# A sorted gather-transform-scatter on one core: 16-bit bank offsets for TensorE's registers, output matmuls four columns later, and no copy behind the sort

## The chip, the cores and the metric

The kernel runs on one core of one Trainium2 chip. The metric is the device time in microseconds (us) of one execution; before the change its median over three runs is 989.48 us, with 987.77 us the lowest and 990.58 us the highest.

A core has a matrix engine (TensorE, "PE" in the profile; its weight loads are listed apart as "PEld"), a vector engine (VectorE, "DVE"), a scalar engine (ScalarE, "ACT"), GpSimd ("POOL") and SyncE ("SP", used here to issue DMAs). Each engine takes its instructions in order from a queue of its own; a small processor in front of each engine, its sequencer, reads that queue and itself executes the instructions that work on registers. Engines wait for one another through semaphores. PSUM is the memory that TensorE writes into, SBUF the memory that all engines read and write.

## What is computed

There are 4096 nodes with 256 features each and 262,144 edges. Each edge adds the transformed features of its source node to its destination node; each node also gets its own transform.

```python
def reference(nodes, edges_src, edges_dst, w_msg, w_self):
    N, D = nodes.shape
    self_out = nodes @ w_self
    src_feat = nodes[edges_src]
    msg = src_feat @ w_msg
    agg = np.zeros((N, D), dtype=np.float32)
    np.add.at(agg, edges_dst, msg)
    return (self_out + agg).astype(np.float32)
```

## The kernel before

The kernel turns the scatter into dense matrix products. It has three stages.

**Transform.** `Y = nodes @ w_msg` is computed once per block of 128 nodes (line 182) and kept in SBUF in bfloat16 as 32 blocks of 128 rows. The transposed nodes stay in SBUF as `XT`.

**Sort.** The 262,144 edges are packed as one number each: the group of 512 destination nodes (a "segment", 8 of them), then the block of 128 source nodes (32 of them), then the destination within the segment and the source within the block. A bitonic network sorts these keys in `_run_sort`. Two layouts are used, "A" (tiles `XA`) and "B" (tiles `XB`), each with two buffers; every pass reads one buffer and writes the other, so that an index `cur` tells which of the two holds the live data. A pass is two VectorE instructions, a minimum (line 574) and a maximum (line 575). Changing the layout goes through TensorE transposes and PSUM (`switch_A_to_B`, `switch_B_to_A`). After the last pass the function makes sure that the result lies in buffer 0 of each layout (lines 598 to 604), because the code behind it names `XA[0]` and `XB[0]`. Layout A has 111 passes, an odd number, so that its live buffer is the second one and the copy on line 599 runs; layout B has 60, so that its own copy never appears in the program. The last `switch_A_to_B` stands between the two.

**Count and apply.** The sorted edges form 2048 columns of 128. For each column, VectorE has built two one-hot matrices (function `onehots`, line 307, 16 columns at a time): one for the source within its block (`e_oh`, 128 wide) and one for the destination within a window of 96 nodes (`d_oh`). Their product on TensorE (`count_mm`, line 323) counts edges between each source and destination, and adds into PSUM. A (segment, block) pair is called a run; there are 256 runs, 8 columns each on average, and six of them share PSUM at a time as a ring of six banks of 512 columns (`ring`). Where in the ring a column's 96-wide window lies is known only after the sort: it is the column's "offset". The offsets are computed on VectorE as `poff` (line 238), go to DRAM (`pd`, line 239) and come back as one row of 2048 numbers on one partition (`poffs`, line 240). TensorE's sequencer loads eight of them into registers with one instruction (line 396, `TENSOR_LOAD` in the profile), and every count matmul has an instruction of its own that turns its register into a PSUM address (`FUSED_REGOPS` in the profile, also put down to line 323).

The order of TensorE's queue in this stage is written out by hand under `tc.manual_schedule()`. For column `c`: at `c % 16 == 0` the one-hots are requested; a run's first columns may need an additional count matmul (`head_mm`, one for each run); at `c % 8 == 0` the eight offsets are loaded; then comes the count matmul. When all columns that can belong to run `r` are past (`8*r + 7 + MARG <= c`, with `MARG` 10), ScalarE copies the run's bank to SBUF as bfloat16 (`evac`, line 339), and `LAG` columns later the four output matmuls of the run follow (`apply_run`, line 365), which multiply the counts by the block of `Y` and add into `out_ps`. The first run of a segment has eight more matmuls for the node's own transform (line 360), and the last one copies `out_ps` to `o_sb` on ScalarE (line 372) and sends it to DRAM from SyncE's queue.

```python
            if c % 8 == 0:
                regs = [nc.tensor.alloc_register(f"po{c}_{i}") for i in range(8)]
                nc.tensor.load(regs, poffs[0:1, c:c + 8])
            off = nc.tensor.snap(
                regs[c % 8], donate=True, min_val=0, max_val=RING * SEGW - W
            )
            count_mm(ring[:, bass.ds(off, W)], e, d, ci, False)
            while nev < NRUN and (8 * nev + 7 + MARG <= c or c == NCOL - 1):
                evac(nev)
                todo.append((c + LAG, nev))
                nev += 1
            while todo and (todo[0][0] <= c or c == NCOL - 1):
                apply_run(todo.pop(0)[1])
```

Everywhere else a scheduler puts VectorE's, ScalarE's and the DMA instructions in order. Around the end of the sort VectorE's queue also holds a check that the sorted data fits the fixed windows (lines 416 to 446: `bad`, `bcol`, `bsum`, `flag`), and the index `cidx` (line 264) with which GpSimd fetches the columns for the head matmuls (line 273).

Of the kernel before, what the change touches and what calls it, by code (L numbers as in the profile page):

```python
# [9 lines left out]
P = 128  # L10
FP32 = mybir.dt.float32
BF16 = mybir.dt.bfloat16
I32 = mybir.dt.int32
I64 = mybir.dt.int64

ALU = mybir.AluOpType
AX = mybir.AxisListType
# [4 lines left out]
SL = 16  # L22
RING = 6
MARG = 10
LAG = 10
NRUN = 256
SENT = float((1 << 24) - 1)

# [7 lines left out]
def _view3(ap: bass.AP, inner: int):  # L36
    return ap.rearrange("p (a b) -> p a b", b=inner)
# [3 lines left out]
def kernel(  # L41
# [9 lines left out]
    nc = tc.nc  # L51
# [4 lines left out]
    NCOL = E // P  # L56
# [3 lines left out]
    NSTAGE = 18  # L60
    JBITS = 11
    G16 = NCOL // P
# [3 lines left out]
    meta = ctx.enter_context(tc.tile_pool(name="meta", bufs=1))  # L66
    dram = ctx.enter_context(tc.tile_pool(name="dram", bufs=1, space=bass.MemoryType.DRAM))
# [2 lines left out]
    xs_dram = dram.tile([NCOL, P], FP32, name="xs_dram")  # L70
    kd = dram.tile([1, NCOL + 1], FP32, name="kd")
    gd = dram.tile([1, NCOL], FP32, name="gd")
    pd = dram.tile([1, NCOL], I32, name="pd")
    fd = dram.tile([1, P], FP32, name="fd")
    rd = dram.tile([1, NCOL + 64], I32, name="rd")

    ident = const.tile([P, P], FP32, name="ident")
# [8 lines left out]
    XA = [sortp.tile([P, NCOL], FP32, name=f"XA{i}") for i in range(2)]  # L86
    XB = [sortp.tile([P, NCOL], FP32, name=f"XB{i}") for i in range(2)]

    HC = NCOL // 2
    for h in range(2):  # L90
        d64 = XB[0][:].bitcast(I64)
        s64 = XB[1][:].bitcast(I64)
        nc.sync.dma_start(
# [14 lines left out]
            out=key, in0=dlo, scalar=128.0, in1=slo, op0=ALU.mult, op1=ALU.add  # L108
        )
        nc.vector.scalar_tensor_tensor(  # L110
            out=key, in0=dhi, scalar=float((1 << 21) - (1 << 16)), in1=key,
# [3 lines left out]
            out=key, in0=shi, scalar=float((1 << 16) - P), in1=key,  # L115
# [24 lines left out]
        out=hbase[:], in0=hbase[:], scalar1=float(SEGW), scalar2=None, op0=ALU.mult  # L140
# [6 lines left out]
        out=thr[:], in0=thr[:], scalar1=float(SEGW), scalar2=-0.5, op0=ALU.mult, op1=ALU.add  # L147
# [31 lines left out]
    for t in range(T):  # L179
        y_ps = psum_y.tile([P, D], FP32, name="y_ps", tag="y_ps", bufs=2)  # L180
        for k in range(2):
            nc.tensor.matmul(  # L182
                out=y_ps[:], lhsT=XT[:, k, t * P:(t + 1) * P], rhs=wcat[:, 2 + k, :],
# [2 lines left out]
        nc.scalar.copy(out=Y[:, t, :], in_=y_ps[:])  # L186

    psum_sort = tc.alloc_tile_pool(name="psum_sort", bufs=1, space=bass.MemoryType.PSUM)
    _run_sort(nc, psum_sort, XA, XB, ident, NCOL, NSTAGE, JBITS, G16)
    srt = XA[0]  # L190
    lane = XB[0]


    k16 = meta.tile([P, G16], FP32, name="k16")
# [9 lines left out]
    gb = meta.tile([P, G16], FP32, name="gb")  # L204
    sl = meta.tile([P, G16], I32, name="sl")
    wr = meta.tile([P, G16], I32, name="wr")
    poff = meta.tile([P, G16], I32, name="poff")
    gball = meta.tile([P, NCOL], FP32, name="gball")
    poffs = meta.tile([1, NCOL], I32, name="poffs")
    junk = meta.tile([P, NCOL], BF16, name="junk")  # L210
    cnt = meta.tile([P, 2], FP32, name="cnt")
    cidx = meta.tile([P, 2], I32, name="cidx")
# [8 lines left out]
        out=ex[:], in0=dl[:], scalar1=float(W - SEGW), scalar2=0.0, op0=ALU.add, op1=ALU.max  # L221
# [9 lines left out]
        out=wr[:], in0=sl[:], scalar1=float(RING), scalar2=float(-RING * SEGW),  # L231
# [3 lines left out]
        out=wr[:], in0=sl[:], scalar=float(SEGW), in1=wr[:], op0=ALU.mult, op1=ALU.add  # L235
# [20 lines left out]
    for h in range(2):  # L256
        nc.scalar.activation(
            out=junk[:], in_=gball[:], func=ACTF.Sign, bias=thr[:, h:h + 1], scale=-1.0,
# [3 lines left out]
        out=cnt[:], in0=cnt[:], scalar1=0.5, scalar2=float(NCOL // 2 - 1), op0=ALU.mult, op1=ALU.add  # L262
    )
    nc.vector.tensor_scalar(
        out=cidx[:], in0=cnt[:], scalar1=0.0, scalar2=None, op0=ALU.max
# [5 lines left out]
    for h in range(2):  # L271
        xh = meta.tile([P, P], FP32, name=f"xh{h}")
        nc.gpsimd.indirect_dma_start(
            out=xh[:], out_offset=None, in_=xs_dram[:, :],
# [61 lines left out]
    def evac(r):  # L336
        at = ohp.tile([P, SEGW], BF16, name="at", tag="at", bufs=4)
        b = (r % RING) * SEGW
        ins = nc.scalar.copy(out=at[:], in_=ring[:, b:b + SEGW]).ins  # L339
        tc.declare_no_dep(  # L340
            ins, group="count", keep=[last_mm[0]], reason="disjoint banks by static schedule"
        )
        tc.add_manual_dep(ins, last_mm[0].name, DEP, reason="run complete")
        tc.add_to_no_dep_group("evac", ins)
        evac_of[r] = ins
        at_of[r] = at
# [28 lines left out]
    with tc.manual_schedule():  # L375
# [5 lines left out]
        for c in range(NCOL):  # L381
# [19 lines left out]
# [4 lines that stand above are left out]
# [18 lines left out]
        out=hh[:], in0=rho[:], scalar1=float(SEGW), scalar2=float(SEGW), op0=ALU.mult, op1=ALU.add  # L423
    )
    nc.vector.scalar_tensor_tensor(
        out=v[:], in0=gn[:], scalar=1.0, in1=hh[:], op0=ALU.add, op1=ALU.min
# [3 lines left out]
        out=bad[:], in0=v[:], scalar=float(W), in1=bad[:], op0=ALU.is_gt, op1=ALU.add  # L430
# [3 lines left out]
        out=bad[:], in0=v[:], scalar=float(W - 1), in1=bad[:], op0=ALU.is_gt, op1=ALU.add  # L434
# [4 lines left out]
        out=bad[0:1, 0:1], in0=gi[0:1, 0:1], scalar=float(W - 1), in1=bad[0:1, 0:1],  # L439
# [16 lines left out]
def _any_edges(tc, edges_src, edges_dst, out, XT, Y, wcat, ident, N, D, E, T):  # L456
    nc = tc.nc
    with tc.tile_pool(name="g_sb", bufs=1) as sb, tc.tile_pool(
# [14 lines left out]
        with tc.For_i(0, E, P) as i:  # L473
            s64 = sb.tile([P, 1], I64, name="g_s64")
            d64 = sb.tile([P, 1], I64, name="g_d64")
            nc.sync.dma_start(s64[:], edges_src[bass.ds(i, P)].unsqueeze(1))
# [34 lines left out]
def _run_sort(nc, psum, XA, XB, ident, NCOL, NSTAGE, JBITS, G16):  # L511

    cur = {"A": 0, "B": 0}

    def buf(lay):
        return XA[cur[lay]][:, 0:NCOL] if lay == "A" else XB[cur[lay]][:, 0:NCOL]

    def other(lay):
        return XA[1 - cur[lay]][:, 0:NCOL] if lay == "A" else XB[1 - cur[lay]][:, 0:NCOL]

    def flip_live(lay):
        cur[lay] = 1 - cur[lay]

    def evac(out_ap, in_ap, g):
        if g % 2 == 0:
            nc.scalar.copy(out=out_ap, in_=in_ap)  # L526
        else:
            nc.vector.tensor_copy(out=out_ap, in_=in_ap)

    def switch_A_to_B():  # L530
        src = buf("A")
        dst3 = buf("B").rearrange("q (p g) -> q p g", g=G16)
        for g in range(G16):
            tp = psum.tile([P, P], FP32, name="tp_sw", tag="tp", bufs=4)
            nc.tensor.transpose(tp[:], src[:, g * P:(g + 1) * P], ident[:])  # L535
            evac(dst3[:, :, g], tp[:], g)

    def switch_B_to_A():
        src3 = buf("B").rearrange("q (p g) -> q p g", g=G16)
        dst = buf("A")  # L540
        for g in range(G16):
            tp = psum.tile([P, P], FP32, name="tp_sw2", tag="tp", bufs=4)
            nc.tensor.transpose(tp[:], src3[:, :, g], ident[:])
            evac(dst[:, g * P:(g + 1) * P], tp[:], g)

    def flip(lay, blo, bhi):
        x = buf(lay)
        if lay == "A":
            assert blo <= JBITS - 1 and (bhi is None or bhi <= JBITS - 1)
            base_lo = blo  # L550
        else:
            assert blo >= 7
            base_lo = blo - 7
            if bhi is not None:
                assert bhi == blo + 1
        if bhi is None:
            per = 1 << (base_lo + 1)
            reg = _view3(x, per)[:, :, (1 << base_lo):per]
        else:
            per = 1 << (base_lo + 2)  # L560
            reg = _view3(x, per)[:, :, (1 << base_lo):(3 << base_lo)]
        nc.vector.tensor_scalar(out=reg, in0=reg, scalar1=-1.0, scalar2=None, op0=ALU.mult)

    def cpass(lay, fb):
        src = buf(lay)
        dst = other(lay)
        per = 1 << (fb + 1)
        s3 = _view3(src, per)
        d3 = _view3(dst, per)
        lo_s = s3[:, :, 0:(1 << fb)]  # L570
        hi_s = s3[:, :, (1 << fb):per]
        lo_d = d3[:, :, 0:(1 << fb)]
        hi_d = d3[:, :, (1 << fb):per]
        nc.vector.tensor_tensor(out=lo_d, in0=lo_s, in1=hi_s, op=ALU.min)  # L574
        nc.vector.tensor_tensor(out=hi_d, in0=lo_s, in1=hi_s, op=ALU.max)  # L575
        flip_live(lay)

    for s in range(1, NSTAGE + 1):
        if s <= JBITS - 1:
            if s == 1:  # L580
                flip("A", 1, None)
            else:
                flip("A", s - 1, s)
            for b in range(s - 1, -1, -1):
                cpass("A", b)
        else:
            switch_A_to_B()
            if s == NSTAGE:
                flip("B", NSTAGE - 1, None)
            else:  # L590
                flip("B", s - 1, s)
            for b in range(s - 1, 6, -1):
                cpass("B", b - 7)
            switch_B_to_A()
            for b in range(6, -1, -1):
                cpass("A", b)

    if cur["A"] != 0:
        nc.vector.tensor_copy(out=XA[0][:, 0:NCOL], in_=XA[cur["A"]][:, 0:NCOL])
        cur["A"] = 0  # L600
    switch_A_to_B()
    if cur["B"] != 0:
        nc.vector.tensor_copy(out=XB[0][:, 0:NCOL], in_=XB[cur["B"]][:, 0:NCOL])
        cur["B"] = 0


# [28 lines left out]
```

## Time and profile before

| | |
|---|---|
| median of three runs | 989.48 us |
| the profiled execution, its own time | 990.0 us |
| its span, first to last instruction | 988.2 us |
| mean granted TensorE clock | 0.846 of full speed |
| PE busy | 417.9 us (42%), 3730 matmuls |
| DVE busy | 782.6 us (79%) |
| ACT busy | 222.0 us (22%) |
| DMA | 18.03 MB, mean 18 GB/s |

The page has six parts: busy time per engine, the span in 40 slices, the DMA queues, the chain of work that ended last, the costliest groups of instructions, and the DMA issues. The sort fills the span up to about 518 us, with VectorE busy nearly all the time. The count stage runs from about 548 us to the end. In a group's row stand line, engine, operation, destination and sources, then count, busy time and mean duration of one in nanoseconds, and last the idle time of the engine just before these instructions and what ended it; "issue" is idle time that ended without any wait that the profile shows.

### The profile page before, as it was taken

Reading aid. Unit: us, or ns where it says so; the run is one execution under the profiler, and the core shown is the slowest. Engines: PE = TensorE matmul, PEld = TensorE weight load, DVE = VectorE, ACT = ScalarE, POOL = GpSimd, SP = SyncE. Lnnn points to the kernel's source line nnn. Section 1 sums busy time; section 2 is a strip of 40 time slices with the busy share of each in tenths; the row PEclk is TensorE's granted clock in tenths of the full one; section 3 lists DMA queues with packets and bytes.
Section 4 is the critical chain, followed back from the end, with each engine's and each line's share of the span. In section 5 each row is a group of like instructions: output and inputs, shape, how many; then the busy total and the mean of one; then the engine's idle time right before and its main releaser. Section 6 shows DMA issues by size and latency. Waiting matters only on the chain.

```text
span 988.2 us, 11711 instructions
## 1 busy us (share of the span) xinstructions
PE 417.9 (42%) x3730; PEld 317.9 (32%) x3730; DVE 782.6 (79%) x851; ACT 222.0 (22%) x449; POOL 14.3 (1%) x24
## 2 busy tenths in 40 slices
PE   0033301131111120202012677777777777777775
PEld 0000001121111120101011566565565656566654
DVE  3999999989999989898995986767766666767640
ACT  0011101021010110101003233333333333333333
POOL 4000000000000000000000000000000000000000
PEclk9999999999555555555555699999999999999999
DMA  8611100000000000000003000000000000000000
GB/s 228 132 26 26 24 0 0 1 1 0 0 0 0 0 1 0 0 0 0 0 0 93 1 2 23 1 23 1 1 23 2 23 1 23 2 23 1 23 2 24
DMA packets 25217, 18.03 MB, mean 18 GB/s; under 512 B 11557, under 2 KB 24358, under 8 KB 24390
## 3 DMA queue, kind: packets, MB, share of 16 engines
q1 hardware_dynamic: 19862, 11.59, 3.9%
q0 software_dynamic: 4720, 2.49, 1.9%
q10 hardware_dynamic: 578, 3.16, 0.8%
q8 instruction: 39, 0.64, 0.3%
q14 instruction: 18, 0.15, 0.0%
HBM read 10.12 MB, written 7.37 MB: 18 GB/s over the span
## 4 chain that ended last, share of the span: by engine, by line
DVE 49%; PE 35%; issue 12%; DMA 3%; ACT 0%; DVEq 0%; ACTq 0%; SPq 0%
PE ring L323 18%; PE out_ps L365 10%; DVE XA_85 L574 7%; DVE XA_84 L574 7%; DVE XA_85 L575 7%; DVE XA_84 L575 6%; DVE XB_86 L574 4%; DVE XB_87 L574 4%; DVE XB_87 L575 3%; DVE XB_86 L575 3%; PE tp_sw L535 3%; DVE e_oh L307 2%; DVE d_oh L307 2%; DMA XB_86<-in_edges_dst_dram 2%; DMA fd<-bcol 1%
## 5 line engine op out<-in xcount | busy, mean ns | idle before, releaser
L323 PE MATMUL ring<-d_oh,e_oh 128*128 128x96 bf16 x2304 | 242.3, 206 | 114.9 <-issue 105.0
L307 DVE TENSOR_TENSOR e_oh<-slo_b,jrow 128x2048 bf16<-128x2048 bf16 x128 | 156.5, 1222 | 114.1 <-PE ring L323 114.1
L323 PEld LDWEIGHTS <-e_oh 128*128 128x128 bf16 x2304 | 170.2, 98 | 158.9 <-issue 143.5
L339 ACT CAST at<-ring 128x512 bf16<-128x512 f32 x256 | 150.0, 586 | 289.9 <-PE ring L323 289.9
L365 PE MATMUL out_ps<-Y,at 128*128 128x256 bf16 x1024 | 154.3, 273 | 0.2 <-ACT at L339 0.2
L307 DVE TENSOR_TENSOR d_oh<-rel_b,jrow 128x1536 bf16<-128x1536 bf16 x128 | 121.7, 951 | 0.0
L365 PEld LDWEIGHTS <-at 128*128 128x128 bf16 x1024 | 85.0, 97 | 15.9 <-issue 1.8
L574 DVE TENSOR_TENSOR XA_85<-XA_84 128x1024 f32<-128x1024 f32 x56 | 68.6, 1225 | 2.2
L574 DVE TENSOR_TENSOR XA_84<-XA_85 128x1024 f32<-128x1024 f32 x55 | 67.4, 1225 | 2.2
L575 DVE TENSOR_TENSOR XA_85<-XA_84 128x1024 f32<-128x1024 f32 x56 | 68.3, 1219 | 0.0
L575 DVE TENSOR_TENSOR XA_84<-XA_85 128x1024 f32<-128x1024 f32 x55 | 67.1, 1219 | 0.0
L182 PE MATMUL y_ps<-wcat,XT 128*128 128x256 bf16 x64 | 25.2, 395 | 97.5 <-DMA XT<-nodes_bf_dram 97.5
L535 PE MATMUL tp_sw<-ident,XA_84 128*128 128x128 f32 x80 | 20.6, 432 | 88.1 <-DVE XA_84 L575 68.9
L535 PE MATMUL tp_sw<-ident,XA_85 128*128 128x128 f32 x64 | 15.8, 436 | 93.7 <-DVE XA_85 L575 93.7
L535 PEld LDWEIGHTS tp_sw<-ident,XA_84 128*128 128x128 f32 x80 | 14.1, 192 | 94.5 <-DVE XA_84 L575 70.0
L182 PEld LDWEIGHTS <-XT 128*128 128x128 bf16 x64 | 6.7, 104 | 115.7 <-DMA XT<-nodes_bf_dram 115.7
L535 PEld LDWEIGHTS tp_sw<-ident,XA_85 128*128 128x128 f32 x64 | 11.6, 190 | 97.8 <-DVE XA_85 L575 52.4
L526 ACT COPY XB_86<-tp_sw 128x128 f32<-128x128 f32 x40 | 15.1, 377 | 119.4 <-PE tp_sw L535 116.9
L574 DVE TENSOR_TENSOR XB_87<-XB_86 128x1024 f32<-128x1024 f32 x30 | 36.8, 1225 | 1.0
L574 DVE TENSOR_TENSOR XB_86<-XB_87 128x1024 f32<-128x1024 f32 x30 | 36.8, 1225 | 1.0
L575 DVE TENSOR_TENSOR XB_87<-XB_86 128x1024 f32<-128x1024 f32 x30 | 36.6, 1219 | 0.0
L575 DVE TENSOR_TENSOR XB_86<-XB_87 128x1024 f32<-128x1024 f32 x30 | 36.6, 1219 | 0.0
(478 smaller groups left out, 288.3 us busy)
## 6 DMA issues: line engine op xcount, KB each, us to landing
out_dram<-o_sb SPq DMA_DIRECT2D x16, 256.0 KB, 2.5
XB_87<-in_edges_src_dram ACTq DMA_DIRECT2D x2, 1024.0 KB, 8.7
XB_86<-in_edges_dst_dram SPq DMA_DIRECT2D x2, 1024.0 KB, 8.5
nodes_bf<-in_nodes_dram POOLq DMA_DIRECT2D x1, 2048.0 KB, 20.1
nodes_bf_dram<-nodes_bf SPq DMA_DIRECT2D x1, 2048.0 KB, 8.7
XT<-nodes_bf_dram SPq DMA_TRANSPOSE x64, 2.4
xs_dram<-XA_84 ACTq DMA_DIRECT2D x1, 1024.0 KB
gball<-gd SPq DMA_DIRECT2D x1, 1024.0 KB, 4.7
```

The source lines that it names most:

```text
L182: nc.tensor.matmul(out=y_ps[:], lhsT=XT[:, k, t * P:(t + 1) * P], rhs=wcat[:, 2 + k, :], start=(k == 0), stop=(k == 1),)
L307: tt(out=o[:], in0=val.rearrange("p (g i) -> p g i", i=2).unsqueeze(2).to_broadcast(shp), in1=jrow[:, 0:wid, :].unsqueeze(1).to_broadcast( ...
L323: mm = nc.tensor.matmul(out=ap, lhsT=e[:, ci // 2, :, ci % 2], rhs=d[:, ci // 2, :, ci % 2], start=start, stop=True, skip_group_check=True ...
L339: ins = nc.scalar.copy(out=at[:], in_=ring[:, b:b + SEGW]).ins
L365: nc.tensor.matmul(out=out_ps[:, t, :], lhsT=at[:, t * P:(t + 1) * P], rhs=Y[:, b, :], start=False, stop=(b == T - 1), skip_group_check=True,)
L526: nc.scalar.copy(out=out_ap, in_=in_ap)
L535: nc.tensor.transpose(tp[:], src[:, g * P:(g + 1) * P], ident[:])
L574: nc.vector.tensor_tensor(out=lo_d, in0=lo_s, in1=hi_s, op=ALU.min)
L575: nc.vector.tensor_tensor(out=hi_d, in0=lo_s, in1=hi_s, op=ALU.max)
```

## The change

Three edits are made together. The offsets are kept as 16-bit integers (`poff`, `pd`, `poffs`), so that a load of eight registers reads 16 bytes instead of 32. `LAG` goes from 10 to 14: a run becomes ready for its output matmuls at columns with `c % 8 == 1`, so with 10 they stood behind the count of a column with `c % 8 == 3`, and with 14 they stand behind one with `c % 8 == 7`, directly ahead of the next register load. And `_run_sort` returns the live buffers instead of copying layout A's into buffer 0.

```diff
@@ -12,6 +12,7 @@
 I64 = mybir.dt.int64
+I16 = mybir.dt.int16
@@ -22,7 +23,7 @@
 MARG = 10
-LAG = 10
+LAG = 14
@@ -70,7 +71,7 @@
-    pd = dram.tile([1, NCOL], I32, name="pd")
+    pd = dram.tile([1, NCOL], I16, name="pd")
@@ -186,9 +187,7 @@
-    _run_sort(nc, psum_sort, XA, XB, ident, NCOL, NSTAGE, JBITS, G16)
-    srt = XA[0]
-    lane = XB[0]
+    srt, lane = _run_sort(nc, psum_sort, XA, XB, ident, NCOL, NSTAGE, JBITS, G16)
@@ -204,9 +203,9 @@
-    poff = meta.tile([P, G16], I32, name="poff")
+    poff = meta.tile([P, G16], I16, name="poff")
     gball = meta.tile([P, NCOL], FP32, name="gball")
-    poffs = meta.tile([1, NCOL], I32, name="poffs")
+    poffs = meta.tile([1, NCOL], I16, name="poffs")
@@ -595,13 +594,8 @@
-    if cur["A"] != 0:
-        nc.vector.tensor_copy(out=XA[0][:, 0:NCOL], in_=XA[cur["A"]][:, 0:NCOL])
-        cur["A"] = 0
     switch_A_to_B()
-    if cur["B"] != 0:
-        nc.vector.tensor_copy(out=XB[0][:, 0:NCOL], in_=XB[cur["B"]][:, 0:NCOL])
-        cur["B"] = 0
+    return XA[cur["A"]], XB[cur["B"]]
```

In the changed program TensorE's queue holds the same instructions as before, in the new order. VectorE's queue has one instruction less (the copy); the addition that makes `poff` becomes a plain 16-element one; and the scheduler puts a few small instructions elsewhere: `cidx` goes ahead of seven of the small instructions of the check instead of behind them, and `bsum` goes behind the first dozen one-hot pairs instead of ahead of the first head one-hot. The queues of SyncE, ScalarE and GpSimd keep their order.

## The prediction

> **What bounds the kernel now.** I read the page's busy rows and its chain of waits first, then the rows of groups, then the chain and the timeline of a few microseconds, and last the single lines.
>
> ```profile
> DVE 49%; PE 35%; issue 12%; DMA 3%; ACT 0%; DVEq 0%; ACTq 0%; SPq 0%
> ```
> ```profile
> L323 PE MATMUL ring<-d_oh,e_oh 128*128 128x96 bf16 x2304 | 242.3, 206 | 114.9 <-issue 105.0
> L307 DVE TENSOR_TENSOR e_oh<-slo_b,jrow 128x2048 bf16<-128x2048 bf16 x128 | 156.5, 1222 | 114.1 <-PE ring L323 114.1
> ```
>
> The chain has two halves: VectorE (the sort) and TensorE (the count stage) with 12% of "issue". The count matmuls stand idle 105 us for "issue", that is, for no other engine, while VectorE waits 114 us for them: in the count stage VectorE is not the bound. The chain in the middle of the stage shows the rhythm (start, length, what):
>
> ```profile
> 701.60 0.44 PE out_ps L365 x4
> 702.03 0.22 PE ring L323 x5
> 702.25 0.41 issue
> 702.66 0.57 PE ring L323 x4
> 703.23 0.44 PE out_ps L365 x4
> ```
>
> One run takes 1.63 us: 0.44 for four output matmuls, 0.22 for five counts, a hole of 0.41, 0.57 for four counts. The array needs only 0.44 for the outputs and 9 x 0.044 = 0.40 for the counts (five in 0.22 when they stand ready), 0.84 in all. What fills the rest is in the lines of the sequencer's own instructions (minimum/median/maximum in ns, then first and last start in us; the windows are 700 to 712 us for the second row, one run from 714.1 us for the third):
>
> ```profile
> L396 PEldq TENSOR_LOAD <-poffs x256: 587/591/1332, 548.2 to 977.7; - x128
> ...
> L396 PEldq TENSOR_LOAD <-poffs x8: 587/590/593, 700.2 to 711.8; - x8
> ...
> L323 PEldq FUSED_REGOPS  x8: 37/37/37, 714.2 to 715.0; - x8
> ...
> L451 PEldq TENSOR_LOAD <-flag x1: 307/307/307, 980.9 to 980.9; - x1
> ```
>
> Loads follow each other every (711.8-700.2)/7 = 1.66 us and last 0.59. The eight address instructions behind each start 0.11 to 0.12 apart ((715.0-714.2)/7) although each lasts 0.037, and do so across the four output matmuls as well: output matmuls cost the sequencer nothing that shows. So the sequencer alone has 0.59 + about 0.10 to the first address instruction + 8 x 0.115 + a few hundredths = 1.63, the whole period. The timeline confirms it twice:
>
> ```profile
> 550.90 1.09 PE L323 MATMUL ring<-d_oh,e_oh 128*128 128x96 bf16 x9 [0.58 <-issue]
> 552.56 1.10 PE L323 MATMUL ring<-d_oh,e_oh 128*128 128x96 bf16 x9 [0.57 <-issue]
> ...
> 558.75 0.93 PE L323 MATMUL ring<-d_oh,e_oh 128*128 128x96 bf16 x9
> 559.48 0.88 PE L365 MATMUL out_ps<-Y,at 128*128 128x256 bf16 x4
> 560.20 0.56 PE L323 MATMUL ring<-d_oh,e_oh 128*128 128x96 bf16 x9
> ```
>
> At 551 us there are no output matmuls yet, and the period is 1.66 all the same. At 557 to 561 us the array runs at half clock and is behind; then the hole is gone, but the three loads begun there last 587 to 593 ns: a load neither waits for matmuls that are outstanding nor gets shorter beside them.
>
> **What the Trainium skill says.** "Advanced Engine Details and Errata", Sequencer Loop: engine instructions are pushed into a queue, control instructions run on the sequencer itself; that is what the rows above show. Its Engine Queue Depths gives TensorE 64; the 13 matmuls outstanding at 559.1 us did not fill it. "DMA: Bandwidth & Descriptors", Latency and other measured facts, puts a floor of about 600 ns under a register load; the trace has 590 for eight registers, but 307 for one, so it is no floor. "Runtime: NRT & Kernel Launch", Instruction fetch mechanics, prices a register load from HBM at about 200 ns per register even in bulk; from SBUF the trace has 590/8 = 74. No page says what the element's width does.
>
> **The change part by part.**
>
> *Output matmuls directly ahead of the load.* The same instructions, in the order: nine counts, four outputs, load. The array can do the outputs during the load, but the sequencer must still do its load and its eight address instructions one after the other, and every count waits for its own. The counts that used to pile up behind the outputs and run during the load now come 0.115 apart. The period stays the sum above: I cost the move at 0. A run's copy on ScalarE gets four columns more before its output needs it; it does not wait for that now. The array's 0.84 us fit into any period down to that.
>
> *16-bit loads.* A load then reads 16 bytes instead of 32. The trace does not show such a load. Lower end: the one-register load, 307 ns. Upper end of a harmless outcome: 590. Two readings of 307 and 590: each further register costs (590-307)/7 = 40 ns, and width is nothing; or the load reads memory in blocks, one block for the single register and two for 32 bytes, as 590 is close to twice 307. If the fixed part of a load is between 37 ns (an address instruction) and 100 ns (what passes behind a load), the second block is worth 207 to 270 and each register 2 to 11, and eight registers in one block take 307 + 7 x (2 to 11) = 321 to 384. I take this reading, since 40 ns for each register is a lot for a processor that does a whole address instruction in 37, and the value 370, nearer its careful end: 0.22 us less. All 256 loads are on the path: 256 x 0.22 = 56.3 us. Given back: at half clock (548 to 561 us, clock 0.54) the array needs 1.58 us a run, more than the new 1.41; some five runs at 0.17, 0.8 us.
>
> What is late next? At 1.41 a run VectorE has 2.83 us for 16 columns; its pair takes 2.17 (1.222 + 0.951), 2.0 when pairs overlap (545.79 to 547.79 in the chain), with the heads' share a quarter more: 2.25. ScalarE has 0.59 a run. The array has 0.84. None is the bound.
>
> *The copy at the end of the sort,* and what the scheduler moves with it:
>
> ```profile
> 517.23 1.23 DVE L599 COPY XA_84<-XA_85 128x2048 f32<-128x2048 f32 x1
> ...
> 535.65 0.17 DVE L264 TENSOR_SCALAR cidx<-cnt 128x2 int32<-128x2 f32 x1
> 536.10 1.09 POOL L273 DMA_INDIRECT xh_1583<-xs_dram,cidx  x1 [522.91 <-DVE cidx L264]
> ...
> 545.52 0.27 DVE L445 TENSOR_REDUCE bsum<-brow 1x1 f32<-1x128 f32 x1 [0.36 <-DMA brow<-fd]
> 545.72 1.20 DVE L307 TENSOR_TENSOR e_oh<-hsl,jrow 128x2048 bf16<-128x2048 bf16 x1
> ```
>
> Everything behind the copy waits for it: with its gap 1.26 us (517.23 to 518.49). `cidx`, from which the fetch of the head columns starts, goes ahead of seven small instructions 0.21 apart: 1.4 us earlier, and the chain cidx, fetch, transpose, head one-hots sets when TensorE starts counting. `bsum`, for which VectorE waited 0.36 and which stood ahead of the first head one-hot, goes behind: 0.57 us (545.15 to 545.72). Sum 3.2 us, at least the 1.26. The halved offset transfers (issued at 521.8 and 523.9 us) are wanted at 548.2 and stay hidden. At the end of the run one more output group falls into the last column, where the array waits for ScalarE anyway: 0.
>
> **Sum.** 990.0 (the profiled execution, 1.8 around its span) - 56.3 + 0.8 - 3.2 = 931.3; the median of the runs shown is 0.5 below that execution, so I forecast 931.
>
> **The rivals.**
>
> *Width is nothing* (10%): the load stays at 590. Then only the 3.2 us come: 986. For it: a load that works register by register would scale with their number, and 40 ns is possible. This lies at the limit of 0.3% (3 us, about what a measurement here can tell), so half of it counts as no change.
>
> *The move hides the load* (3%): the hole of 0.41 goes altogether, 256 x 0.41 + 3.2 = 108 us, 882. Against it: the sequencer is in order, and the 551 us rows keep 1.66 without any output matmul.
>
> *16-bit values are not read in blocks* (17%): a load of narrow elements, which must be widened to a register, could go element by element. Place: TensorE's sequencer, line 396. Price: seven further accesses of 200 ns (the runtime page's, and the 207 to 270 above), 307 + 1400 = 1.7 us a load, 1.1 more than now, 256 x 1.1 = 286, to 1273; with 307 for each register it is 2.46 us and 1465. It decides as soon as a load takes more than 590 + 6200/256 = 614 ns. For it speaks that nothing here shows a 16-bit load; against it that 74 ns per register shows that this load does read more than one register at a time.
>
> **How the numbers follow.** The main case has 70%. Its own range: a load of 321 ns gives 918, one of 450 (a widening cost of 10 ns for each register on top) gives 951. The range must leave out no more than 20%: the third rival (17%) and the second (3%) stay out, the first is taken in, and a little is added below: 912 to 990. Faster by over 0.3%: 70 + 3 + 5 = 78%; within 0.3%: 5%; slower: 17%.
>
> **What would show it.** The load's row is the test: about 370 ns right, 590 or more wrong. Loads should follow each other every 1.41 to 1.44 us, the hole before the first count of a run should still stand, now behind the outputs, and the address instructions should still be 0.115 apart. If the period falls below the sum of load and address instructions, I am wrong about the sequencer; if it stays above it, something else (VectorE's one-hots first) has become late. Line 599 should be gone and the first load should begin near 545 us.

## The result, and the profile after

The changed kernel takes 1324.85 us (median of four runs, 1323.69 to 1325.13) against 988.99 us for the kernel before in the same comparison: a ratio of 1.339, with a 95% interval of 1.337 to 1.342. It is slower by 336 us. The profiled execution took 1325.13 us, its span is 1323.4 us.

The rows of groups of the changed kernel, to be held against those of before:

```profile
L306 DVE TENSOR_TENSOR e_oh<-slo_b,jrow 128x2048 bf16<-128x2048 bf16 x128 | 156.7, 1224 | 426.8 <-PE ring L322 426.8
L322 PE MATMUL ring<-d_oh,e_oh 128*128 128x96 bf16 x2304 | 278.2, 247 | 269.3 <-issue 145.8
```

VectorE does the same work as before (156.7 us in this row) but now waits 427 us for TensorE instead of 114. TensorE waits for "issue" in 146 of its 269 us. Most of the rest (116) is put down to `e_oh`, but that is not what it waited for: at 902.16 us, for one, the hole is again 1.03 us, and the one-hot instruction named had ended at 901.55. The sequencer's own lines say what the wait is for. They are the register loads of the whole program, the eight address instructions of one run, and the single-register load of `flag`, each with minimum/median/maximum in ns and then first and last start in us:

```profile
L395 PEldq TENSOR_LOAD <-poffs x256: 1916/1919/2555, 546.3 to 1310.7; - x128
...
L322 PEldq FUSED_REGOPS  x8: 37/37/37, 913.9 to 914.8; - x8
...
L450 PEldq TENSOR_LOAD <-flag x1: 320/320/320, 1315.1 to 1315.1; - x1
```

A 16-bit load of eight registers takes 1919 ns where the 32-bit load took 591. The address instructions are untouched (37 ns, 0.9/7 = 0.13 us apart at this rounding), and a load of one 32-bit register still takes about 0.3 us. The chain of waits in the middle of the stage shows what is left of the rhythm (start, length, what):

```profile
908.13 1.07 PE ring L322 x9
909.20 0.85 PE out_ps L364 x4
910.05 1.03 issue
911.09 0.98 PE ring L322 x8
```

One run takes 911.09 - 908.13 = 2.96 us. The output matmuls do stand ahead of the load, as the change wants, and a part of the load does pass beside them; what sticks out behind them is 1.03 us in which the array has nothing to do. The stage runs at half the array's clock (0.52 between 600 and 1200 us), and that does not set the time: even so the array has run out of work 1.03 us before the next address is ready. The arithmetic closes: 256 loads x (1.919 - 0.591) = 340 us, against 336 measured.

### The profile page after: what moved, and what is told of

Read it like the earlier page. It is cut to its first block, busy times and chain, and to the rows that moved or that the text cites. A ratio compares the mean times of both kernels' runs of the same rounds, so it can differ in the third digit from the quotient of the medians.

```text
span 1323.4 us, 11701 instructions
## 1 busy us (share of the span) xinstructions
PE 600.9 (45%) x3730; PEld 420.8 (32%) x3730; DVE 782.3 (59%) x850; ACT 222.2 (17%) x449; POOL 14.4 (1%) x24
## 4 chain that ended last, share of the span: by engine, by line
DVE 45%; PE 35%; issue 17%; DMA 2%; ACT 0%; POOL 0%; DVEq 0%
PE ring L322 21%; DVE e_oh L306 11%; PE out_ps L364 9%; DVE XA_85 L573 5%; DVE XA_84 L573 5%; DVE XA_85 L574 5%; DVE XA_84 L574 5%; DVE XB_87 L573 3%; DVE XB_86 L573 3%; DVE XB_86 L574 3%; DVE XB_87 L574 3%; PE tp_sw L534 2%; DMA XB_86<-in_edges_dst_dram 1%; PE out_ps L359 1%; DVE d_oh L306 1%
## 5 line engine op out<-in xcount | busy, mean ns | idle before, releaser
L306 DVE TENSOR_TENSOR e_oh<-slo_b,jrow 128x2048 bf16<-128x2048 bf16 x128 | 156.7, 1224 | 426.8 <-PE ring L322 426.8
L322 PE MATMUL ring<-d_oh,e_oh 128*128 128x96 bf16 x2304 | 278.2, 247 | 269.3 <-issue 145.8
L322 PEld LDWEIGHTS <-e_oh 128*128 128x128 bf16 x2304 | 236.9, 117 | 373.4 <-issue 337.5
L364 PE MATMUL out_ps<-Y,at 128*128 128x256 bf16 x1024 | 264.1, 412 | 0.0
L364 PEld LDWEIGHTS <-at 128*128 128x128 bf16 x1024 | 124.5, 137 | 33.7
```

The lines of the kernel that those rows point to most:

```text
L306: tt(out=o[:], in0=val.rearrange("p (g i) -> p g i", i=2).unsqueeze(2).to_broadcast(shp), in1=jrow[:, 0:wid, :].unsqueeze(1).to_broadcast( ...
L322: mm = nc.tensor.matmul(out=ap, lhsT=e[:, ci // 2, :, ci % 2], rhs=d[:, ci // 2, :, ci % 2], start=start, stop=True, skip_group_check=True ...
L364: nc.tensor.matmul(out=out_ps[:, t, :], lhsT=at[:, t * P:(t + 1) * P], rhs=Y[:, b, :], start=False, stop=(b == T - 1), skip_group_check=True,)
```

## The experiments

The expectations name a theory A and its rivals. At first A says only that narrow elements are fetched register by register; ahead of the runs with a spread and a shifted row it is widened: only a contiguous, aligned row of full-width elements is fetched several registers at a time, and anything else goes register by register. The sequencer's sum (load + 0.1 us + eight address instructions) then gives the time.

**One part alone: 16-bit offsets.**

```diff
-    pd = dram.tile([1, NCOL], I32, name="pd")
+    pd = dram.tile([1, NCOL], I16, name="pd")
...
-    poff = meta.tile([P, G16], I32, name="poff")
+    poff = meta.tile([P, G16], I16, name="poff")
...
-    poffs = meta.tile([1, NCOL], I32, name="poffs")
+    poffs = meta.tile([1, NCOL], I16, name="poffs")
```

> The kernel before with the 16-bit offsets alone (poff, pd and poffs as 16-bit integers; LAG stays 10, the copy stays). Theory A (a load of narrow elements fetches each register by an access of its own, 307 + 7 x 230 = 1917 ns, and TensorE's sequencer is the bound): loads of 1917 to 1922 ns, one load every 2.95 us, 1325 to 1330 us in all. Rival B (the narrow load is slow only because the output matmuls now stand directly ahead of it): loads near 590 or below, 930 to 990 us.

It took 1325.75 us against 990.25 for the kernel before, ratio 1.339 (1.337 to 1.341), the ratio of the whole change. Its load line:

```profile
L397 PEldq TENSOR_LOAD <-poffs x256: 1916/1919/2227, 546.6 to 1310.1; - x128
```

The output matmuls stand at their old place here, and the load is just as long. The 16-bit edit is the whole loss; rival B falls.

**The rest of the change without it.** The changed kernel with the three tiles back at 32 bits (LAG 14, no copy):

```diff
-    pd = dram.tile([1, NCOL], I16, name="pd")
+    pd = dram.tile([1, NCOL], I32, name="pd")
...
-    poffs = meta.tile([1, NCOL], I16, name="poffs")
+    poffs = meta.tile([1, NCOL], I32, name="poffs")
```

> The changed kernel with the offsets back at 32 bits: LAG 14 and no copy. Theory A: loads at 590 ns, 1.63 us a run, and only the earlier start of the count stage is left, 2 to 3 us: 985 to 987. Rival C (the move by four columns costs something of its own in the count stage): above 990. Rival D (the move hides the load behind the output matmuls): 880 to 950.

986.27 us against 990.25: ratio 0.9958 (0.9944 to 0.9972), with loads of 590 ns. The size is what theory A expected, but not the place: the first load begins at 548.1 us, where it began before (548.2), and the next two runs divide the gain differently.

**The move alone.**

```diff
-LAG = 10
+LAG = 14
```

> The kernel before with LAG 14 alone. Theory A: no change, 988 to 990, one load every 1.63 to 1.64 us with the hole now behind the output matmuls instead of behind five counts. Rival C: above 992. Rival D: 880 to 950.

986.89 us, ratio 0.9964 (0.9951 to 0.9978): 3.4 us faster, where theory A had nothing. The main point of A holds; the chain of waits of this run:

```profile
702.02 0.44 PE out_ps L365 x4
702.46 0.18 issue
702.64 1.01 PE ring L323 x9
703.65 0.44 PE out_ps L365 x4
```

The hole has shrunk from 0.41 to 0.18 us, as one would hope when work is put beside a load, and the run still takes 703.65 - 702.02 = 1.63 us. What the hole lost came back in the counts: nine now take 1.01, where five that had piled up and four at the sequencer's pace took 0.22 + 0.57 = 0.79. Idle time of the array moved; the sum on the sequencer did not. The 3.4 us come from elsewhere. The load line names a place:

```profile
L396 PEldq TENSOR_LOAD <-poffs x256: 587/590/932, 549.6 to 975.6; - x128
```

The longest load is 932 ns; before it was 1332. Before, seven loads, one at each change of segment, took about 1.2 us, while the output of the last segment leaves (`out_dram<-o_sb`). From the first to the last load 426.0 us pass instead of 429.5; about 2.2 of these 3.5 us lie in the two intervals between loads at each change, the rest is spread over the others. That the loads now meet less of the output transfer fits, but no run separates the transfer from the other work of a change of segment, so this stays an inference. Nor does the move always help there: with 16-bit loads, usually 1.92 us, those at the changes last 2.36 to 2.56 us with `LAG` 14 and 2.20 to 2.23 with `LAG` 10.

**The copy alone.** The kernel before, with `_run_sort` returning the live buffers and nothing else.

```diff
-    if cur["A"] != 0:
-        nc.vector.tensor_copy(out=XA[0][:, 0:NCOL], in_=XA[cur["A"]][:, 0:NCOL])
-        cur["A"] = 0
     switch_A_to_B()
...
+    return XA[cur["A"]], XB[cur["B"]]
```

> The kernel before without the copy at the end of the sort, nothing else; VectorE's queue keeps bsum ahead of the first head one-hot. If the copy stands on the path to the end (prediction): 1.2 us less than before, or more. If the fetches through DRAM behind it set the start of the count stage instead: 0 to 0.7 us less.

989.12 us, ratio 0.9998 (0.9988 to 1.0009): nothing that can be measured. The timeline of this run between the sort and the counts (start, length, engine, line, operation, idle time before):

```profile
517.12 0.17 DVE L216 CAST k16i<-XA 128x16 int32<-128x16 f32 x1
...
534.70 0.32 SPq L442 DMA_DIRECT2D fd<-bcol  x1
...
542.31 0.24 SPq L443 DMA_DIRECT2D brow<-fd  x1
...
545.57 0.27 DVE L444 TENSOR_REDUCE bsum<-brow 1x1 f32<-1x128 f32 x1 [0.82 <-DMA brow<-fd]
545.77 1.20 DVE L306 TENSOR_TENSOR e_oh<-hsl,jrow 128x2048 bf16<-128x2048 bf16 x1
```

The first instruction behind the sort starts 1.37 us earlier (518.49 before), and the transfer of `bcol` is issued 0.87 earlier (535.57 before), but the first head one-hot starts at 545.77 against 545.72. In front of it stands `bsum`, which waits for a round trip through DRAM (`fd`, `brow`): 10.9 us from issue to `bsum` here, 9.95 before. Why the round trip took longer in this execution is open; one trace of each kernel cannot tell. In the changed kernel, and in the run with 16-bit offsets alone, the scheduler puts `bsum` further back (568.1 and 568.2 us); there the first load begins at 546.3 and 546.6 instead of 548.2, without the copy and with it.

**Is it the width of the element or the length of the row?** Loads of four 32-bit registers, 16 bytes like the changed kernel's.

```diff
-            if c % 8 == 0:
-                regs = [nc.tensor.alloc_register(f"po{c}_{i}") for i in range(8)]
-                nc.tensor.load(regs, poffs[0:1, c:c + 8])
+            if c % 4 == 0:
+                regs = [nc.tensor.alloc_register(f"po{c}_{i}") for i in range(4)]
+                nc.tensor.load(regs, poffs[0:1, c:c + 4])
...
-                regs[c % 8], donate=True, min_val=0, max_val=RING * SEGW - W
+                regs[c % 4], donate=True, min_val=0, max_val=RING * SEGW - W
```

> The kernel before with 32-bit loads of four registers each, twice as many loads: 16 bytes a load, as many as the changed kernel reads. Theory A with blocks of 16 bytes (a contiguous 32-bit row is fetched block by block): a load of 310 to 350 ns, two of them and two gaps of 0.1 in place of one, 0.1 to 0.2 us more a run, 1015 to 1040 us. Rival E (width of the row, not of the element, makes a 16-byte load slow): a load of 900 ns or more, over 1200 us. Rival F (each register 40 ns, no blocks): a load of 427 ns, 0.36 us more a run, about 1083 us.

```profile
L396 PEldq TENSOR_LOAD <-poffs x512: 326/328/772, 548.6 to 1023.2; - x171
```

328 ns for four registers, 21 more than for one (7 each), and 262 less than for eight. So three more registers cost 21 ns and the next four 262. That fits blocks of four registers, 16 bytes; no run loads five or six, so the step itself is not seen. A short row is not slow: rivals E and F fall. The time, 1033.97 us (ratio 1.044, 1.043 to 1.046), follows from twice as many loads.

**Is it narrowness, or anything that is not a plain row?** First the same 32-bit values spread out, one every 8 bytes:

```diff
-    poffs = meta.tile([1, NCOL], I32, name="poffs")
+    poffs = meta.tile([1, NCOL, 2], I32, name="poffs")
...
-    nc.scalar.dma_start(poffs[:], pd[0:1, :])
+    nc.scalar.dma_start(poffs[:, :, 0], pd[0:1, :])
...
-                nc.tensor.load(regs, poffs[0:1, c:c + 8])
+                nc.tensor.load(regs, poffs[0:1, c:c + 8, 0])
```

> The kernel before with the 32-bit offsets spread out in SBUF, one every 8 bytes, so that a load's eight values are full width but not contiguous; values and order as before. Theory A in its wide form (block fetches only for a contiguous row of 32-bit elements; anything else goes register by register): loads of 1915 to 1925 ns, about 1325 us. Rival G (only narrow elements go one by one; a strided row is still fetched in 16-byte blocks, four of them): 307 + 3 x 234 + 7 x 7 = 1058 ns, about 1110 us. Rival H (each needed block of 16 bytes costs nothing more, the load stays at 590): 990 us.

Then the plain row, shifted by one element:

```diff
-    poffs = meta.tile([1, NCOL], I32, name="poffs")
+    poffs = meta.tile([1, NCOL + 1], I32, name="poffs")
...
-    nc.scalar.dma_start(poffs[:], pd[0:1, :])
+    nc.scalar.dma_start(poffs[:, 1:NCOL + 1], pd[0:1, :])
...
-                nc.tensor.load(regs, poffs[0:1, c:c + 8])
+                nc.tensor.load(regs, poffs[0:1, c + 1:c + 9])
```

> The kernel before with the row of 32-bit offsets shifted by one element, so that every load starts 4 bytes behind a multiple of 16. Theory A in its wide form with alignment as a condition: 1915 to 1925 ns, about 1325 us. Rival I (unaligned rows are read in three blocks): 307 + 2 x 234 + 7 x 7 = 824 ns, about 1050 us. Rival H: 590 ns, 990 us.

Their load lines, the spread row first:

```profile
L396 PEldq TENSOR_LOAD <-poffs x256: 1920/1926/2217, 554.5 to 1319.3; - x128
```
```profile
L396 PEldq TENSOR_LOAD <-poffs x256: 1929/1933/2228, 548.8 to 1315.8; - x128
```

1926 and 1933 ns, 1333.64 and 1330.17 us (one execution each; the spread row's first load begins 7.9 us later than that of the run with 16-bit offsets alone, and the same 7.9 us lie between their times). Narrow, spread or shifted, a load of eight costs the same, to within 1%. That speaks for one common slow path: 16-bit elements do not have a slow way of their own, they lose the fast one. Rivals G, H and I fall. If each register is fetched on its own there, a further register costs (1919 - 307)/7 = 230 ns; that it is so is argued and not shown, since every slow load here has eight registers.

**Fewer, longer loads.** The second run's kernel with 32 registers per load, and with 16; each 8 in these lines becomes 32 or 16. The edit for 16:

```diff
-            if c % 8 == 0:
-                regs = [nc.tensor.alloc_register(f"po{c}_{i}") for i in range(8)]
-                nc.tensor.load(regs, poffs[0:1, c:c + 8])
+            if c % 16 == 0:
+                regs = [nc.tensor.alloc_register(f"po{c}_{i}") for i in range(16)]
+                nc.tensor.load(regs, poffs[0:1, c:c + 16])
...
-                regs[c % 8], donate=True, min_val=0, max_val=RING * SEGW - W
+                regs[c % 16], donate=True, min_val=0, max_val=RING * SEGW - W
```

> The kernel of the second run (LAG 14, no copy, 32-bit) with 32 registers per load, a quarter of the loads. Theory A with blocks (234 ns for a further 16 bytes, 7 ns for a further register): 307 + 7 x 234 + 31 x 7 = 2162 ns a load, 0.49 us less for each 32 columns, 64 times: 32 us less than 986, 952 to 957. Rival F (no blocks, 40 ns a register): 1547 ns, about 915. If something other than the sequencer is close behind, less than 20 us come.

> The kernel of the second run (LAG 14, no copy, 32-bit) with 16 registers per load. From the loads measured so far (328 ns for 4, 590 for 8, 2131 for 32: about 231 for each further 16 bytes and 7 for each register) a load takes 307 + 3 x 231 + 15 x 7 = 1105 ns, 16 columns 3.09 instead of 3.27 us, 128 times: 23 us less than 986, about 963, if the hole of about 0.8 us in TensorE's work leaves its clock up, as the 2 us hole with 32 registers did not (clock 0.90 in that stage). If the clock falls here too, 970 to 980.

```profile
L395 PEldq TENSOR_LOAD <-poffs x64: 2126/2131/3027, 547.2 to 958.4; - x64
```
```profile
L395 PEldq TENSOR_LOAD <-poffs x128: 1101/1104/2001, 547.6 to 960.6; - x128
```

The loads come out as expected, 2131 ns (2162 expected) and 1104 (1105). The times do not: 974.69 us with 32 registers, ratio 0.9843 (0.9826 to 0.9859), where 952 to 957 was expected, and 974.33 us with 16, ratio 0.9839 (0.9826 to 0.9852), where 963 was expected as long as the clock stays up. Both kernels are faster than the kernel before, but against 986.27 us the gain is 12 us each, where the shorter loads alone would give 32 with 32 registers and 23 with 16. With 16 registers the clock stays up, so the doubt stated ahead of that run is not the reason:

```profile
600.00:900.00 300.00, 233.69 (x2440) 190.72 (x2440) 215.07 (x209) 113.54 (x196) 0.00 (x0) 0.99 0.04 12
...
710.09 1.03 PE L359 MATMUL out_ps<-wcat,XT 128*128 128x256 bf16 x8 [0.63 <-ACT o_sb L371]
...
L322 PEldq FUSED_REGOPS  x7: 37/37/37, 708.5 to 709.2; - x7
...
L395 PEldq TENSOR_LOAD <-poffs x1: 2001/2001/2001, 710.1 to 710.1; - x1
```
```profile
608.49 1.03 PE L360 MATMUL out_ps<-wcat,XT 128*128 128x256 bf16 x8
```

The first line is 600 to 900 us of that kernel (busy time of PE, PEld, DVE, ACT, POOL, then clock 0.99, DMA share and GB/s). The second is the start of a segment: its first output matmul now waits 0.63 us for ScalarE's copies of the segment before, where the kernel before had no such wait (its line stands by itself, at 608.49 us). The third and fourth are the sequencer's address instructions ahead of that point and its next load.

In this run most loads follow each other every 3.09 to 3.26 us, but at the seven changes of segment two intervals in a row reach 3.5 to 4.2; that is 1.2 to 1.8 us a change and 11 in all, where the second run's kernel loses 4. Two things add up there, at all seven changes. The sequencer stands: its load begins only when the matmul that waited for ScalarE begins (both at 710.1, the last address instruction before at 709.2), 0.83 to 0.98 us after the last address instruction has ended, where 0.08 is usual. And the load itself then lasts 1.45 to 2.00 us instead of 1.10. So 7 of the 11 us that are missing with 16 registers lie at the changes of segment; the other 4 are not traced. With 32 registers the changes lose 13 to 14 us and the clock is also down, 0.90; how much the clock takes there is not settled.

**Half the loads by packing two offsets in one word.** VectorE computes `odd * 4096 + even`; eight registers serve 16 columns, and the sequencer takes the pair apart.

```diff
...
+            if c % 2 == 0:
+                two = nc.tensor.snap(regs[c % 16 // 2], donate=True, min_val=0, max_val=(1 << 24) - 1)
+                off = (two & 4095).with_bounds(min_val=0, max_val=RING * SEGW - W)
+            else:
+                off = (two >> 12).with_bounds(min_val=0, max_val=RING * SEGW - W)
```

> The kernel of the second run with two 12-bit offsets packed in one 32-bit word by VectorE and taken apart again on TensorE's sequencer (a mask for the even column, a shift inside the address instruction for the odd one): eight registers serve 16 columns, half of the loads. Theory A: loads stay at 590 ns, which saves 0.69 us for each 16 columns, 88 us; the mask is one more sequencer instruction for every second column, 1024 of them, at 0.04 to 0.1 us, 41 to 102 us: 940 to 1000 us. If the masks hide behind what already separates two address instructions, near 900.

1039.06 us, ratio 1.050 (1.048 to 1.052), above the 940 to 1000 that I expected. The loads are as expected, 590 ns and half as many. The sequencer's lines over 16 columns, between two loads:

```profile
L326 PEldq FUSED_REGOPS  x16: 42/58/73, 711.2 to 714.7; - x16
L326 PEldq ALU_OP  x8: 32/32/32, 711.5 to 714.9; - x8
```

The mask is an instruction of its own, and the address instruction with the shift lasts 73 ns instead of 37. Loads follow each other every 3.74 us (median) instead of 2 x 1.63, although one load and the 0.1 us behind it, 0.69 us, are saved: the unpacking costs 0.69 + 0.47 = 1.16 us for 16 columns, 0.145 for each pair. I had priced the mask alone.

## Why the prediction was wrong

**What bounds the kernel** was right, and carried through every run: the sequencer's sum of load, 0.1 us and eight address instructions gave the period of all of them in which the load alone changed, to within 6% and apart from the changes of segment. With 1.919 in place of 0.591 it gives 1.63 + 1.33 = 2.96, and 2.96 was measured.

**The 16-bit loads** are the step that failed. I read 307 and 590 ns as blocks, one and two, and the load of four registers bears that out: 328 ns, 7 ns a register, inside the 2 to 11 that I had worked out. What I then did was to let a row of 16-bit elements count as one block, at 370 ns, where the trace had only 32-bit rows to show. Measured is 1919: a narrow row does not get the block reading at all, and costs what a spread or a shifted row costs. The term was not mis-sized, it had the wrong sign: -56 us forecast, +340 shown.

**The rival that came true** was the third, with its place (the sequencer, the load's line) and its price right: 1273 to 1465 forecast, 1325 measured. If the load does go register by register, a further register costs 230 ns. The low end of my price was the 200 that the Trainium skill gives for a register load from HBM ("Runtime: NRT & Kernel Launch", Instruction fetch mechanics), though these loads come from SBUF; the high end was 307. I gave it 17%. The argument that I held against it, 74 ns per register, spoke of the 32-bit load only; it could not tell how narrow elements are read. For an operation that no trace shows, the choice between two mechanisms should not have become 70 to 17.

**The move** was costed at 0 and gave 3.4 us. That it leaves the period in the middle of a segment at 1.63 us was right and is shown by the run with it alone. The larger part of the gain, 2.2 us, sits at the changes of segment, which I had not looked at.

**The copy and what moves with it** were costed at 3.2 us, at least 1.26. The copy alone gave nothing measurable. I had seen that `bsum` and its wait stand ahead of the first head one-hot, but took the transfer that it waits for to move up with the rest. In the run with the copy alone taken out it was issued 0.87 us earlier, and `bsum` began at 545.57 us against 545.52. What the changed kernel gains at the start of the count stage, 548.2 - 546.3 = 1.9 us, it gains almost whole with the copy still in place (546.6), and not at all with the copy gone and 32-bit tiles (548.1, `bsum` at its old place). So it comes with the scheduler's new order, which the 16-bit tiles brought, and not from the copy.

**What is late next** came to no test in the changed kernel. In the kernels with longer loads it was the change of segment: there TensorE waits for ScalarE's copies of `out_ps`, while I had priced only ScalarE's one copy for each run.

## What to carry to other kernels

Where an engine shows "issue" holes at a regular distance, add up its sequencer's own instructions: if they fill the period, moving other work beside a hole moves idle time and leaves the period as it is. Keep the values that TensorE's sequencer loads as 32-bit elements in a contiguous row, with each load a multiple of 16 bytes from the start of its tile, the form that was fast here; as 16-bit elements the load of eight took more than three times as long. Longer loads helped a little: 16 registers at a time gave 12 us, and 32 no more than that. An instruction that no trace shows in the form meant should be measured alone before a kernel is built on it.

## What the runs showed of the hardware that was not expected

Register loads from SBUF on TensorE's sequencer, in ns: one 32-bit register 307, four 328, eight 590, sixteen 1104, thirty-two 2131; that is 257 to 262 for every further four registers. Eight registers from 16-bit elements 1919, from every second element 1926, from a row 4 bytes off 1933.

With a hole of 1.03 us in every 2.96 us the array's granted clock in the count stage is 0.52; with 32 registers per load, where the holes are 0.4 to 1.8 us, about one every 6.2 us, it is 0.90; with 0.7 us holes every 3.1 us it is 0.99, and with 0.41 us in every 1.63 us 1.00. No run changes the hole alone, so these are four observations and no rule.

A register load does not wait for matmuls that are only outstanding (590 ns with 13 of them in the kernel before), but it stood, 0.83 to 0.98 us, behind a matmul that itself waited for ScalarE, at all seven changes of segment with 16 registers per load.
